# The output's sums of squares and spread roots as products of high and low parts, one dense step later

## The chip, the cores and the metric

The kernel runs on one core of one Trainium2 chip. The metric is device microseconds of one launch, the median of several runs. Beside the runs one execution was profiled; its own time is named beside the median wherever a sum is made from its durations.

## What is computed

One layer of a bidirectional encoder, applied to two requests with the same weights: a prompt of 2048 tokens and a sample of 512, with 16 meta tokens ahead of each. In float32:

```python
def rms_norm(x, g):
    x32 = x.astype(jnp.float32)
    y = x32 * lax.rsqrt(jnp.mean(x32 * x32, axis=-1, keepdims=True) + RMS_EPS)
    return (y * g.astype(jnp.float32)).astype(x.dtype)
...
    u = rms_norm(h, norm_g)
    proj = u @ w_in
    qa, ka, va, za, qb, kb, vb, zb, ga, gb = jnp.split(proj, cuts, axis=-1)
...
    y_a = (o_a * jax.nn.silu(za)) @ w_proj_a
    y_b = (o_b * jax.nn.silu(zb)) @ w_proj_b
    merged = jax.nn.sigmoid(ga) * y_a + jax.nn.sigmoid(gb) * y_b
    return merged @ w_out
...
    h = h + mixer_layer(h, ...)
    return rms_norm(h[:, N_META:], final_g)
```

Here o_a is a neighbourhood attention over a grid of 64 columns and o_b an attention in a window of 128 tokens, each with the meta tokens as extra keys. What matters for the change is the last line: every token's 1024 output features are divided by their root mean square, so that the sum of squares of a token has to be known before any of its features can be written.

## The kernel before, in words

The 2560 tokens are five windows of 512 tokens (w = 0 is the sample, 1 to 4 the prompt). Activations lie feature-major: 128 features on the partitions, 512 tokens along the free dimension, eight such tiles (KT = 8) for 1024 features.

A float32 product is made here in one of two ways. The large ones go through TensorE in its type f32r with both operands split into a high part (a copy that is rounded to f32r) and a low part (the rest): `mm3` at lines 145 to 148 issues high by high, high by low and low by high. `split` (line 251) makes such a pair, ScalarE the high part and VectorE the low one. A few small products are plain f32 (`sums`, line 166, and `spread`, line 181).

First come the input projections, then attention, unit by unit, with dense work in between. Attention units of kind a and of kind b alternate by window: for each window first the 32 units of a, then 16 of b. The unit functions are generators, whose stages are: loads; scores and exponentials (L1111 and L1112 or L1217 and L1218 on TensorE, L1042 on VectorE, L1049 on ScalarE); division by the sum (L1060, L1058); transposes (L1135, or L1237 and L1240) with a split of what they give (L1244, L1245); products with the values (L1150 and L1152, or L1261, L1264 and L1266) and their evacuation (L1268 on ScalarE, the adds of y at L1271 on VectorE). The result of a unit has one PSUM bank (pool ps_o). When a head pair's y is complete, GpSimd multiplies it with the gate (L1274) and it is split into yb (L1066 on ScalarE, L1067 on GpSimd).

The loop over the units (at the end of the kernel) writes out TensorE's order by hand: between the stages `fill` takes so many steps from the queue of dense work. A dense step is the piece of a generator between two `yield`s, six products of 512 columns. The other engines' orders, SP's included, are planned by the compiler's own simulation at build time; `tc.issue_after` puts a limit on that plan.

The dense work of a window w - 1 runs in the units of window w, by `phases` (line 1478): in the a units `dense_pb` and the first half of `dense_out`, in the b units the second half of `dense_out`, then `dense_pa(w)` and, interleaved with it by `with_fill` (line 1470), `dense_fin(w - 1)`. So `dense_fin` runs for four of the five windows. The last window ends otherwise (`finish_end`).

- `dense_pa` and `dense_pb` (lines 1298 and on): psa and psb, the projections of the two branches, eight tiles of two dense steps each. A tile loads its gate (`gated`, line 1293: a DMA on SP into one of three buffers with the tag sg) and multiplies the gate with the PSUM result (ta at L1311). Every two tiles one tile of weights is taken, and the next one is split, the low part on GpSimd (L207, L208).
- `dense_out` (line 1333): pso, the output projection, eight tiles of four dense steps. A tile loads the residual x into an sg buffer (xres), adds it (hT), lets ScalarE square the sum into that same sg buffer and GpSimd add the squares up in one tile ssq of 128 x 512 (L1351, L1353).
- `dense_fin` (line 1355): what is left is the sum over the 128 partitions of ssq, and that goes through TensorE. `sums` uses ssq as weights, 128 tokens at a time, and a column of ones as the moving operand, so that the sums of 512 tokens come out as 128 x 4 (L170). `rsqrt` takes the root by twelve short VectorE instructions (L153 to L163). To bring the roots back to all partitions, `diagonal` (L177) puts each on the diagonal of a 128 x 128 block, and `spread` multiplies by a matrix of ones (L185). ScalarE copies the result to rbs, GpSimd multiplies each of the eight tiles hT with it (L1367), and SP writes them out.

The first piece of `dense_fin` runs with the third dense step of `dense_pa`, then follow five empty steps, then the spread and a tile of the output with each step. TensorE's pool ps_p has three banks with the tag tp; they serve transposes, a third of the a scores, fin_v and rs_rb. The pool d keeps the sg buffers, one buffer with the tag rbs, which holds the diagonal and after it rbs, and one with the tag ssq.

`prep_ahead`, earlier in the kernel, already makes such a sum and spread for other tokens from high and low parts, with `by_ones` (line 188): two products of 512 columns with a matrix of ones as weights (L191, L192).

Of the kernel before, what the change touches and what calls it, by code (L numbers as in the profile page):

```python
# [9 lines left out]
F32 = mybir.dt.float32  # L10
F32R = mybir.dt.float32r
# [6 lines left out]
P = 128  # L18
# [7 lines left out]
WTOK = 512  # L26
# [69 lines left out]
def encoder_block(ctx: ExitStack, tc: tile.TileContext, xT, x_end, w_in, w_pa, w_pb, w_o, norm_g, final_g,  # L96
                  final_row, bias_a0, bias_a1, bias_a2, bias_a3, bias_b, bias_b0, outT_p, outT_s, out_e):
    nc = tc.nc
# [23 lines left out]
    def f32(ap):  # L122
        return ap.bitcast(F32)
# [4 lines left out]
    ones_r = const.tile([P, P], F32R, name="ones")  # L128
# [12 lines left out]
    def move(out, in_):  # L141
        last_move[0] = nc.sync.dma_start(*(f32(a) if a.dtype == F32R else a for a in (out, in_)))
        return last_move[0]
# [6 lines left out]
    def rsqrt(small, sq, m, nc_):  # L150

        ve, hv, r, t = (small.tile([P, 8], F32, tag=f"rs{i}", name=f"rs{i}")[:m, :nc_] for i in range(4))
        nc.vector.tensor_scalar(ve, sq, 1.0 / D_MODEL, EPS, ALU.mult, ALU.add)  # L153
        nc.vector.tensor_scalar(r.bitcast(I32), ve.bitcast(I32), 1, None, ALU.arith_shift_right)
        nc.vector.tensor_scalar(r.bitcast(I32), r.bitcast(I32), -1.0, float(0x5F3759DF), ALU.mult, ALU.add)
        nc.vector.tensor_scalar(hv, ve, -0.5, None, ALU.mult)
        for _ in range(3):
            if nc_ == 1:
                nc.vector.scalar_tensor_tensor(t, r, hv, r, ALU.mult, ALU.mult)
            else:  # L160
                nc.vector.tensor_mul(t, r, hv)
                nc.vector.tensor_mul(t, t, r)
            nc.vector.scalar_tensor_tensor(r, t, 1.5, r, ALU.add, ALU.mult)  # L163
        return r

    def sums(ssq, c0, m, nc_, psum, tag):

        v = psum.tile([P, WTOK], F32, tag=tag, name="fin_v")
        for c in range(nc_):
            nc.tensor.matmul(v[:m, c : c + 1], ssq[:, c0 + c * m : c0 + (c + 1) * m], ones[:, 0:1],  # L170
                             start=True, stop=True)
        return v[:m, :nc_]

    def diagonal(dg, r, m, eng=nc.vector):

        nc_ = r.shape[1]
        eng.tensor_mul(dg[:m, : nc_ * m].rearrange("p (c n) -> p c n", n=m),  # L177
                             ident[:m, None, :m].broadcast_to([m, nc_, m]),
                             r[:m, :, None].broadcast_to([m, nc_, m]))

    def spread(psum, tag, dg, m, nc_):

        rb = psum.tile([P, WTOK], F32, tag=tag, name="rs_rb")
        for c in range(nc_):
            nc.tensor.matmul(rb[:, c * P : c * P + m], ones[:m, :], dg[:m, c * m : c * m + m], start=True, stop=True)  # L185
        return rb

    def by_ones(psum, tag, h, l, name):

        v = psum.tile([P, WTOK], F32, tag=tag, name=name)  # L190
        nc.tensor.matmul(v, ones_r, h, start=True, stop=False)  # L191
        nc.tensor.matmul(v, ones_r, l, start=False, stop=True)  # L192
        return v
# [16 lines left out]
    def split_w(raw, engines=()):  # L210

        wt = wpool.tile([P, 2, KT * P], F32R, tag="wt", name="wt")
        for i, c in enumerate(range(0, KT * P, 4 * P)):
            split_part(wt[:, 0, c : c + 4 * P], wt[:, 1, c : c + 4 * P], raw[:, c : c + 4 * P], *engines[i : i + 1])
        return wt

    class Weights:
# [12 lines left out]
        def split(self, i):  # L230
            if i < len(self.srcs):
                self.wt[i] = split_w(self.raw.pop(i))
# [1045 lines left out]
    pools = {}  # L1278
# [12 lines left out]
    acc = {}  # L1291
# [61 lines left out]
                nc.gpsimd.tensor_add(ssq, ssq, x)  # L1353

    def dense_fin(w):
        r = rsqrt(pools["d"], sums(acc["s", w], 0, P, 4, ps_p, "tp"), P, 4)
        dg = pools["d"].tile([P, WTOK], F32, tag="rbs", name="rs_dg", bufs=1)
        diagonal(dg, r, P)
        for _ in range(5):
            yield  # L1360
        rb = spread(ps_p, "tp", dg, P, 4)
        rbs = pools["d"].tile([P, WTOK], F32, tag="rbs", name="rbs", bufs=1)
        nc.scalar.copy(rbs, rb)
        for f in range(KT):
            hT = acc["h", w, f]
            with tc.issue_after(low[0]):
                nc.gpsimd.tensor_mul(hT, hT, rbs)  # L1367
            dst = outT_s if w == 0 else outT_p
            c0 = 0 if w == 0 else (w - 1) * WTOK
            move(dst[f * P : (f + 1) * P, c0 : c0 + WTOK], hT)  # L1370
            yield
# [106 lines left out]
    def phases(w, br):  # L1478

        if br == "a":  # L1480
            if w == 0:
                yield from islice(gates, GATES_A)
            else:
                yield from dense_pb(w - 1)
                yield from dense_out(w - 1, range(0, 4))
        elif w == 0:
            yield from gates
            open_dense()
            yield from dense_pa(0)
        else:  # L1490
            yield from dense_out(w - 1, range(4, 8))
            pa = dense_pa(w)
            yield from islice(pa, 1)
            yield from with_fill(pa, dense_fin(w - 1))
# [29 lines left out]
    ps_p = ctx.enter_context(tc.tile_pool(name="ps_p", bufs=3, space=PSUM))  # L1524
# [9 lines left out]
    with tc.manual_schedule(engines={E.PE}):  # L1534
# [22 lines left out]
        for i in range(N):  # L1557
            br, w, _, weight = units[i]
# [128 lines left out]
```

## Time and profile before

| | |
|---|---|
| median of 3 runs | 1888.18 us (1886.59 to 1889.76) |
| span of the profiled execution | 1881.7 us |
| TensorE (PE) busy | 1855.9 us, 99% |
| weight loads (PEld) | 1583.0 us, 84% |
| VectorE (DVE) | 1320.6 us, 70% |
| ScalarE (ACT) | 1145.5 us, 61% |
| GpSimd (POOL) | 730.0 us, 39% |
| dense_fin's sums begin at | 1278.35, 1447.54, 1615.05, 1780.16 us |

A row of the order of time gives the start in us from the span's start, the duration, the engine, the line in the code, the operation and the tiles (out<-in), the shapes, and how many like it follow on each other; in brackets stands how long the engine had been idle and what ended that. A matmul's duration is from its start to the modelled end of its way through the array, and the next one starts before that, so TensorE's rate is read from one start to the next. An f32 product of TensorE shows as two instructions, an f32r product as one. In the tile view three numbers are minimum, median and maximum in ns. PEld is TensorE's weight load, which overlaps its matmuls.

### The profile page before, as it was taken

To read this page: it belongs to the slowest core of one execution; us is meant where nothing else is said; L and a number is where in the kernel's file an instruction comes from. 1 tells how busy PE (TensorE), PEld (TensorE's weight loads), DVE (VectorE), ACT (ScalarE), POOL (GpSimd) and SP (SyncE) were. 2 spreads that over 40 slices of the span, in tenths; PEclk is the share of its full clock that TensorE was granted. 3 is DMA by queue.
4 is the path that set the end of the run, shared out by engine and by line. 5 is a ranking of instruction groups with operands and counts; after the bars stand their busy time and mean duration, and the time that the engine had idled before them with its cause. 6 is when DMAs were issued, how large, how long until landed. Compare 5 with 4: busy or idle time off the path is not lost. (4 is left out here: it accounts for less than half of the span.)

```text
span 1881.7 us, 29782 instructions
## 1 busy us (share of the span) xinstructions
PE 1855.9 (99%) x9797; PEld 1583.0 (84%) x9797; DVE 1320.6 (70%) x2961; ACT 1145.5 (61%) x2528; POOL 730.0 (39%) x558
## 2 busy tenths in 40 slices
PE   8999999999999999999999999999999999999998
PEld 6898888888888888888888888888888888888887
DVE  8886657556477565444457888878787887888874
ACT  6454444444365443444456797797789788878932
POOL 2005443323202233322324435656744763685420
PEclk9999999999999999999999999999999999999999
DMA  7667756544296777744258878977985996798383
GB/s 268 234 175 295 207 171 193 211 175 179 84 348 219 235 216 200 209 138 161 104 197 310 273 217 266 304 213 249 316 280 179 320 315 225 222 311 260 119 299 135
DMA packets 290385, 424.83 MB, mean 226 GB/s; under 512 B 117416, under 2 KB 162040, under 8 KB 288696
## 3 DMA queue, kind: packets, MB, share of 16 engines
q1 hardware_dynamic: 289944, 422.93, 69.5%
q8 instruction: 78, 1.28, 0.3%
q14 instruction: 75, 0.61, 0.1%
q10 hardware_dynamic: 288, 0.01, 0.0%
HBM read 303.46 MB, written 119.39 MB: 225 GB/s over the span
## 5 line engine op out<-in xcount | busy, mean ns | idle before, releaser
L208 POOL TENSOR_TENSOR wt<-wraw,wt 128x512 fp32r<-128x512 f32 x164 | 213.1, 1318 | 265.9 <-ACT wt L207 265.8
L848 PE MATMUL pa<-u,wt 128*128 128x512 f32 x1008 | 242.5, 389 | 0.0
L848 PE MATMUL pa<-u,x 128*128 128x512 f32 x984 | 236.9, 390 | 1.2 <-ACT u L859 1.1
L207 ACT CAST wt<-wraw 128x512 fp32r<-128x512 f32 x312 | 177.9, 619 | 74.8 <-PE mm L148 35.3
L848 PEld LDWEIGHTS pa<-u,wt 128*128 128x128 f32 x1008 | 189.0, 188 | 39.2
L848 PEld LDWEIGHTS pa<-u,x 128*128 128x128 f32 x984 | 184.3, 188 | 40.6 <-ACT u L859 2.2
L819 POOL TENSOR_TENSOR s<-wraw,raw 128x512 f32<-128x512 f32 x40 | 58.3, 1458 | 265.5 <-DVE x L208 265.5
L146 PE MATMUL mm<-u,wt 128*128 128x512 f32 (+2 forms) x416 | 150.4, 362 | 7.8 <-ACT u L334 7.2
L814 POOL TENSOR_TENSOR s<-raw 128x512 f32<-128x512 f32 x40 | 58.3, 1456 | 250.0 <-DMA raw<-in_w_in_dram 245.0
L148 PE MATMUL mm<-u,wt 128*128 128x512 f32 (+2 forms) x416 | 146.6, 352 | 2.4 <-DVE wt L208 2.4
L147 PE MATMUL mm<-u,wt 128*128 128x512 f32 (+2 forms) x416 | 146.6, 352 | 1.3 <-DVE u L335 1.3
L208 DVE TENSOR_TENSOR wt<-wraw,wt 128x512 fp32r<-128x512 f32 x148 | 107.2, 762 | 47.2 <-ACT wt L207 47.0
L848 PE MATMUL pe<-u,wt 128*128 128x512 f32 x504 | 121.3, 390 | 0.0
L848 PE MATMUL pc<-u,wt 128*128 128x512 f32 x504 | 121.1, 389 | 0.0
L848 PE MATMUL pe<-u,x 128*128 128x512 f32 x480 | 115.3, 389 | 0.0
L848 PEld LDWEIGHTS pc<-u,wt 128*128 128x128 f32 x504 | 94.6, 188 | 19.6
L848 PEld LDWEIGHTS pe<-u,wt 128*128 128x128 f32 x504 | 94.4, 188 | 19.6
L1139 DVE TENSOR_TENSOR pl<-tp,ph 128x384 fp32r<-128x384 f32 (+6 forms) x160 | 94.8, 593 | 20.2 <-ACT ph L1138 17.7
L1138 ACT CAST ph<-tp 128x384 fp32r<-128x384 f32 (+6 forms) x160 | 81.7, 510 | 43.4 <-PE tp L1135 41.9
L146 PE MATMUL pso<-mh,wt 128*128 128x512 f32 x256 | 107.1, 418 | 0.0
L827 POOL TENSOR_TENSOR s<-wraw,s 128x512 f32<-128x512 f32 x40 | 55.4, 1384 | 131.6 <-DVE wt L208 126.3
L848 PEld LDWEIGHTS pe<-u,x 128*128 128x128 f32 x480 | 90.1, 188 | 18.7
(258 smaller groups left out, 5017.0 us busy)
## 6 DMA issues: line engine op xcount, KB each, us to landing
wraw<-in_w_in_dram SPq DMA_DIRECT2D x86, 512.0 KB
qa<-evq SPq DMA_DIRECT2D x20, 1024.0 KB
raw<-in_w_in_dram SPq DMA_DIRECT2D x40, 512.0 KB
q<-qa SPq DMA_DIRECT2D x20, 1024.0 KB
wraw<-in_w_o_dram SPq DMA_DIRECT2D x32, 512.0 KB
kbt<-kb SPq DMA_DIRECT2D x32, 384.0 KB
qb<-evq SPq DMA_DIRECT2D x20, 512.0 KB
ka<-evk SPq DMA_DIRECT2D x20, 512.0 KB
```

The source lines that it names most:

```text
L146: nc.tensor.matmul(ps, wh, uh, start=first, stop=False)
L147: nc.tensor.matmul(ps, wh, ul, start=False, stop=False)
L148: nc.tensor.matmul(ps, wl, uh, start=False, stop=last)
L207: nc.scalar.copy(h, r)
L208: low[0] = (eng or lo_eng[0]).tensor_sub(l, r, f32(h)).ins
L814: eng.tensor_add(s1, a21, a22)
L819: eng.tensor_sub(s3, a11, a21)
L827: eng.tensor_sub(s4, a12, s2)
L848: nc.tensor.matmul(ps, wt[:, a, s], u[:, b, kk, :], start=first and kk == 0 and i == 0, stop=kk == 3 and i == 2, skip_group_check=True)
L1138: nc.scalar.copy(ph_[:kb, a], tb)
L1139: nc.vector.tensor_sub(pl_[:kb, a], tb, f32(ph_[:kb, a]))
```

## The change

Only `dense_fin` is changed. The sum of squares is split into high and low parts h and l (a copy on ScalarE, a subtraction on VectorE); then a dense step is let pass. The sums are eight f32r products, for each 128 tokens one with h and one with l as weights and two columns of ones as the moving operand, which add up in PSUM. The root is split likewise (128 x 4), each part gets a diagonal of its own, both on VectorE, and after five more steps `by_ones` spreads them with two products of 512 columns. All that follows, the copy to rbs, the products on GpSimd and the output DMAs, comes one dense step later than before. h and the high diagonal take the buffer rbs, the low diagonal that of ssq, and l one of the three sg buffers, in their rotation. rh and rl are two new small tiles.

```diff
     def dense_fin(w):
-        r = rsqrt(pools["d"], sums(acc["s", w], 0, P, 4, ps_p, "tp"), P, 4)
-        dg = pools["d"].tile([P, WTOK], F32, tag="rbs", name="rs_dg", bufs=1)
-        diagonal(dg, r, P)
+        h = pools["d"].tile([P, WTOK], F32R, tag="rbs", name="ssqh", bufs=1)
+        l = pools["d"].tile([P, WTOK], F32R, tag="sg", name="ssql", bufs=3)
+        split(h, l, acc["s", w])
+        yield
+        v = ps_p.tile([P, WTOK], F32, tag="tp", name="fin_v")
+        for c in range(4):
+            for x in (h, l):
+                nc.tensor.matmul(v[:, 2 * c : 2 * c + 2], x[:, c * P : (c + 1) * P], ones_r[:, 0:2],
+                                 start=x is h, stop=x is l)
+        r = rsqrt(pools["d"], v[:, 0:8:2], P, 4)
+        rh, rl = (pools["d"].tile([P, 8], F32R, tag=f"r{x}", name=f"r{x}")[:, :4] for x in "hl")
+        split(rh, rl, r)
+        dh = pools["d"].tile([P, WTOK], F32R, tag="rbs", name="rs_dg", bufs=1)
+        dl = pools["d"].tile([P, WTOK], F32R, tag="ssq", name="rs_dgl", bufs=1)
+        diagonal(dh, f32(rh), P)
+        diagonal(dl, f32(rl), P)
         for _ in range(5):
             yield
-        rb = spread(ps_p, "tp", dg, P, 4)
+        rb = by_ones(ps_p, "tp", dh, dl, "rs_rb")
         rbs = pools["d"].tile([P, WTOK], F32, tag="rbs", name="rbs", bufs=1)
         nc.scalar.copy(rbs, rb)
```

## The prediction

> **What bounds the kernel now.** I read the page first, then the order of time of TensorE around the four places where dense_fin runs, then the tile views of fin_v, and last VectorE, GpSimd and the DMA issues in the same stretches. The page:
>
> ```profile
> span 1881.7 us, 29782 instructions
> PE 1855.9 (99%) x9797; PEld 1583.0 (84%) x9797; DVE 1320.6 (70%) x2961; ACT 1145.5 (61%) x2528; POOL 730.0 (39%) x558
> ```
>
> TensorE bounds the kernel: its order is written by hand and it is busy for 99% of the span. That share proves little alone, as the ends of matmuls are modelled; I go by start to start. The profiled execution has a span of 1881.7 us; the median of the runs is 1888.18, 6.5 us more, which lie around the span. I sum against the span and carry the difference over to the median. Only TensorE time counts in full; work of other engines counts where TensorE then waits for it.
>
> The first dense_fin, in order of time (start, duration, engine, line):
>
> ```profile
> 1277.01 1.28 POOL L1353 TENSOR_TENSOR ssq<-ssq,xres 128x512 f32<-128x512 f32 x1
> 1277.79 0.27 PE L1240 MATMUL tp<-ident,prs 128*32 128x128 f32 x1
> 1278.35 1.05 PE L170 MATMUL fin_v<-ones,ssq 128*128 128x1 f32 x8 [0.29 <-POOL ssq L1353]
> 1279.27 0.47 PE L146 MATMUL psa<-ya,wt 128*128 128x512 f32 x1
> 1279.58 0.39 PE L147 MATMUL psa<-ya,wt 128*128 128x512 f32 x1
> ```
>
> The four f32 products of the sums show as eight instructions, 0.92 us from the first to the next product, 0.11 each. Ahead of them TensorE stands: GpSimd's last sum of squares ends at 1278.29, TensorE starts at 1278.35. The same place in the other three blocks:
>
> ```profile
> 1446.97 0.27 PE L1240 MATMUL tp<-ident,prs 128*32 128x128 f32 x1
> 1447.54 1.02 PE L170 MATMUL fin_v<-ones,ssq 128*128 128x1 f32 x8 [0.29 <-DVE pms L1255]
> 1614.51 0.27 PE L1240 MATMUL tp<-ident,prs 128*32 128x128 f32 x1
> 1615.05 1.02 PE L170 MATMUL fin_v<-ones,ssq 128*128 128x1 f32 x8 [0.26 <-DVE pms L1255]
> 1779.85 0.27 PE L1240 MATMUL tp<-ident,prs 128*32 128x128 f32 x1
> 1780.16 1.05 PE L170 MATMUL fin_v<-ones,ssq 128*128 128x1 f32 x8
> ```
>
> **The wait that goes.** From L1240 to L170 pass 0.56, 0.57, 0.54 and 0.31 us, together 1.98. A transpose needs some 0.11 of that (the L170 instructions' own spacing), so 4 x 0.11 = 0.44 is work and 1.54 us is standing. After the change the sums come one dense step later, that is, after six dense products and the attention work between; in the first block that attention work still runs at 1281.32 (the L1264 row below), so at least 3.0 us lie between GpSimd's end and the sums. In them a ScalarE cast and a VectorE subtraction must run, priced below at 0.62 and 0.76 us. I take the wait as gone: -1.54 us. TensorE now waits for that subtraction, with the next step's six dense products queued behind; if the cover fails, the standing comes back there (rival 1).
>
> **The sums themselves.** They stay eight products with 128x128 weights, now f32r with two columns instead of one. No row before shows that form; what bounds it is the weight load:
>
> ```profile
> L170 PEld LDWEIGHTS fin_v<-ones,ssq x32: 186/192/192, 1278.4 to 1780.9; 128*128 128x128 f32 x32
> L191 PEld LDWEIGHTS fin_v<-xq,ones x2: 188/188/188, 290.7 to 291.1; 128*128 128x128 f32 x2
> 1281.32 0.28 PE L1264 MATMUL ob<-pms,vms 96*64 96x128 f32 x2
> 1281.44 0.28 PE L1266 MATMUL ob<-pl,vb 128*64 128x256 f32 x1
> ```
>
> L170 loads f32 and L191 f32r, both with 128 columns: 192 against 188 ns. So I take 0.11 us each, no change. The other end: the two L1264 products, f32r with weights of 64 columns, take 0.12 together, 0.06 each; at that rate eight save 8 x 0.05 = 0.4 a block, 1.6 in all (rival 2). Above 0.11 I see no reason.
>
> **The spread.** Eight f32 instructions of 128 columns become two f32r products of 512 columns. The kernel has both forms:
>
> ```profile
> 1292.09 1.05 PE L185 MATMUL rs_rb<-rs_dg,ones 128*128 128x128 f32 x8
> 1292.90 0.47 PE L146 MATMUL psa<-ya,wt 128*128 128x512 f32 x1
> 1293.21 0.39 PE L147 MATMUL psa<-ya,wt 128*128 128x512 f32 x1
> 305.49 0.39 PE L191 MATMUL rs_rb<-rs_dg,ones 128*128 128x512 f32 x1
> 305.72 0.40 PE L192 MATMUL rs_rb<-rs_dg,ones 128*128 128x512 f32 x1
> 305.96 0.39 PE L191 MATMUL rs_rb<-rs_dg,ones 128*128 128x512 f32 x1
> ```
>
> From L185 to L147 pass 1.12 us, of which one dense product takes 0.23 (L191 to L192): the spread costs 0.89. The pair at L191 and L192 takes 0.47. Saved: 0.42 a block, -1.68 us for four, all of it on TensorE.
>
> **What is added beside TensorE.** The split of ssq is a cast (L207's kind) and a subtraction (L208's), the split of the root two small ones, and the second diagonal one more L177:
>
> ```profile
> L207 ACT CAST wt<-wraw 128x512 fp32r<-128x512 f32 x312 | 177.9, 619 | 74.8 <-PE mm L148 35.3
> L208 DVE TENSOR_TENSOR wt<-wraw,wt 128x512 fp32r<-128x512 f32 x148 | 107.2, 762 | 47.2 <-ACT wt L207 47.0
> L177 DVE TENSOR_TENSOR rs_dg<-ident,rs x8: 683/689/1683, 26.9 to 1787.3; 128x512 f32<-128x512 f32 x7, 16x16 f32<-16x16 f32 x1
> L153 DVE TENSOR_SCALAR rs<-fin_v x5: 150/156/161, 44.2 to 1781.3; 128x4 f32<-128x4 f32 x4, 128x8 f32<-128x8 f32 x1
> ```
>
> VectorE: 0.76 + 0.16 + 0.69 = 1.6 us a block; ScalarE: 0.62 and a small copy, about 0.16 like L153, 0.8 us. What stands behind them on both engines is the attention's evacuation, and TensorE waits for the adds of y (L1271), since the output of the attention has one PSUM bank:
>
> ```profile
> 1284.00:1290.00 6.00, 6.00 (x40) 5.32 (x39) 5.90 (x14) 3.93 (x11) 2.55 (x2) 1.00 0.46 121
> 1289.73 0.57 DVE L1271 TENSOR_TENSOR y<-ob,ol 64x128 f32<-64x128 f32 x2
> 1290.91 0.28 PE L1261 MATMUL ob<-ph,vb 128*128 128x256 f32 x1
> ```
>
> The columns of the first row are the stretch, its length, and PE, PEld, DVE, ACT and POOL busy. VectorE is full there (5.90 of 6.00), and the adds end at 1290.30, 0.61 us before TensorE wants the bank. But most of the delay is only an exchange: the root's small steps leave that stretch by a dense step, as the sums do, and the diagonals come after 1290. Lower bound 0 (nothing of it is on TensorE), upper bound all of it, 2.4 us a block (rival 3). I take 0, nearest to the quoted 0.61 of cover. The Trainium skill, TensorE: Matmul & The Clock Gate, Architectural detail, calls ScalarE's and VectorE's queues strict first in, first out, which speaks against the change, since a cast that stands early in the queue holds up the rest until ssq is there; no row here can show that cast.
>
> The dependent chain still fits: the spread moves one dense step later together with the sums, and what is put between them (small copy, small subtraction, one diagonal, about 1.0 us) stands against five dense steps, some 14 us (1278.35 to 1292.09).
>
> **What moves.** The spread, the copy of rbs, eight products on GpSimd and eight output DMAs on SP come a dense step later; a step is (1292.09 - 1278.35) / 5 = 2.75 us. No one in the kernel reads the outputs, and the last are due, by fourteen such steps from 1780.16, at about 1819, long before the end. The two halves and the diagonals take buffers (rbs, ssq) whose former content is read before by what they depend on anyway. GpSimd waits for rbs as it does now, only longer:
>
> ```profile
> 1295.84 2.55 POOL L1367 TENSOR_TENSOR hT<-hT,rbs 128x512 f32<-128x512 f32 x2 [8.74 <-ACT rbs L1363]
> 1315.44 1.29 POOL L1067 TENSOR_TENSOR yb<-y,yb 128x512 fp32r<-128x512 f32 x1 [0.79 <-ACT yb L1066]
> 1319.53 0.39 PE L147 MATMUL psb<-yb,wt 128*128 128x512 f32 x1
> ```
>
> Queued behind it are weight splits and the split of yb, which ends at 1316.73 and is wanted at 1319.53: cover 2.80 us against a delay of 2.75. Upper bound one more product ahead of yb, 2.55 / 2 = 1.3 us; lower bound 0, since GpSimd stands for 8.74 us before and can take a split there. I take 0, as even the full delay fits; the other end is rival 4.
>
> The low part l takes a buffer of the gate loads' three. The gate of output tile 1 then cannot be loaded when ssq's tile 6 is done, as now, but after tile 7, at about 1278.3; SP is held there, as it is now for the next gate:
>
> ```profile
> 1278.33 0.89 SPq L142 DMA_DIRECT2D sga<-ga  x2
> 1284.16 0.68 DVE L1311 TENSOR_TENSOR ta<-psa,sga 128x512 f32<-128x512 f32 x1
> DMA packets 290385, 424.83 MB, mean 226 GB/s; under 512 B 117416, under 2 KB 162040, under 8 KB 288696
> ```
>
> It is wanted at 1284.16, 5.8 us later. Even behind a weight tile of 512 KB, 768 KB at the mean 226 GB/s are 3.5 us: cost 0. The gate of tile 3, which follows in l's own buffer, waits for the sums, but its consumer comes four dense steps after 1284.16: cost 0.
>
> **Sum.** 1.54 + 1.68 = 3.2 us less: span 1878.5, median 1888.2 - 3.2 = 1885.0. About 0.2% is what a measurement of this kernel can tell from no change, 3.8 us: the forecast lies just inside.
>
> **Rivals.** (1) A wait takes the old one's place: the subtraction stands behind other VectorE work and l comes late. For it: VectorE is full near by. Against it: 3.0 us for 1.4 us of work. Gain 1.68 only: 1886.5.
>
> (2) The f32r weights load faster: 1.6 us more, 1883.4. The Trainium skill, same page, Weight-path perf modes, has a fast weight load for 128 weights whose type is not FP32, though its table says no win for fp32 widths; the equal 188 and 192 ns speak against it.
>
> (3) The added work lands on TensorE: VectorE and ScalarE are in arrears by 2.4 us a block, the y adds end late, and the bank is not free. It decides once the arrears exceed the cover, 0.61 us in the first block. Price 4 x 2.4 - 3.2 = +6.4: 1894.6, slower. Against it: the exchange above.
>
> (4) GpSimd's delay of a step eats the cover of yb, and one more product of 1.3 us ahead of it lands on TensorE in the three blocks that have attention after them: 3.9 - 3.2 = +0.7: 1888.9.
>
> (5) The order of VectorE, ScalarE and GpSimd is planned anew from the first dense_fin on, and waits elsewhere go:
>
> ```profile
> 1344.23 0.40 PE L1112 MATMUL s<-kd,q 128*128 128x512 f32 x1
> 1345.58 0.52 PE L1135 MATMUL tp<-ident,pr 128*128 128x128 f32 x3 [0.96 <-DVE pr L1060]
> 1355.77 0.40 PE L1112 MATMUL s<-kd,q 128*128 128x512 f32 x1
> 1357.10 0.52 PE L1135 MATMUL tp<-ident,pr 128*128 128x128 f32 x3 [0.93 <-DVE pr L1060]
> ```
>
> Less 0.23 for the product, TensorE stands for 1.12 and 1.10 us. Both gone: 1882.8. Such waits can as well arise.
>
> **Numbers.** Forecast 0.45, rival 1 0.16, rival 2 0.11, rival 3 0.11, rival 4 0.06, rival 5 0.11. Rivals 2 and 5 are faster by over 0.2%, and so is a quarter of the forecast, where a small extra carries it over 3.8 us: 0.11 + 0.11 + 0.11 = 0.33. Rival 3 is slower: 0.11. The rest, 0.56, is within. The range goes from half a microsecond under rival 5, 1882.3, to rival 4, 1888.9; rival 3 and a few points below are left out.
>
> **What would show it.** TensorE from the last transpose to the first product of the next dense step with no standing at dense_fin, sums at 0.11 each and a pair of spread products at 0.47. Standing at the sums with VectorE as releaser shows rival 1; sums at 0.06 rival 2; ob products held by L1271 rival 3; psb held by L1067 rival 4; L1135 waits gone rival 5. The forecast is wrong if the span is not 2.4 to 3.8 us shorter.

## The result and the profile after

The changed kernel takes 1894.11 us (median of 5 runs, 1893.08 to 1896.19), the kernel before 1889.25 beside it (5 runs, 1886.59 to 1890.27): a ratio of 1.0035, interval 1.0022 to 1.0048. By the ratio it is slower by some 6.6 us (the two medians lie 4.9 us apart, 1.0026, which is inside the interval), where 3.2 us less were forecast. The page after:

```profile
span 1891.7 us, 29739 instructions
PE 1861.6 (98%) x9773; PEld 1584.3 (84%) x9773; DVE 1334.0 (71%) x2973; ACT 1148.9 (61%) x2536; POOL 729.2 (39%) x558
```

This execution took 1893.77 us, 2.1 us more than its span. The profiled execution of before (span 1881.7) was thus a quick one, near 1884, and the 10.0 us between the two spans overstate the loss. Single profiles scatter, too: over all 20 kernels, the stretch up to the first pso, ahead of everything that was changed, ends between 1194.3 and 1200.0 us. Where the 10.0 us lie, cut at the first product of psa, psb and pso of each window (sums over the blocks, in us; worked out from the traces' starts):

| stretch | before | after |
|---|---|---|
| up to the first pso | 1194.3 | 1195.7 |
| dense_fin: psa to psb, 4 blocks | 160.2 | 163.5 |
| units of a: psb to pso, 3 | 126.5 | 128.7 |
| pso to psa, 4 | 324.4 | 326.0 |
| from the fourth block's psb to the end | 76.3 | 77.8 |

**The sums came out as forecast.** The order of time of TensorE in the second block:

```profile
1452.58 0.35 PE L1218 MATMUL s<-kbt,q 128*128 128x402 f32 x1
1452.77 0.17 PE L1363 MATMUL fin_v<-ones,ssqh 128*128 128x2 f32 x1
...
1453.46 0.25 PE L1363 MATMUL fin_v<-ones,ssql 128*128 128x2 f32 x1
1453.58 0.48 PE L146 MATMUL psa<-ya,wt 128*128 128x512 f32 x1
```

No standing ahead of L1363, and eight products in 0.81 us. The tile view of fin_v after gives their weight loads (minimum, median and maximum in ns):

```profile
L1363 PEld LDWEIGHTS fin_v<-ones,ssqh x16: 187/192/192, 1282.4 to 1793.3; 128*128 128x128 f32 x16
```

192 ns, as f32 had.

**The spread did not.** The same view, some 14 us later:

```profile
1463.23 0.28 PE L1261 MATMUL ob<-ph,vb 128*128 128x256 f32 x1
1464.15 0.31 PE L1264 MATMUL ob<-pms,vms 96*64 96x128 f32 x2 [0.64 <-DVE pms L1255]
...
1466.79 0.27 PE L1240 MATMUL tp<-ident,prs 128*32 128x128 f32 x1
1468.13 0.47 PE L191 MATMUL rs_rb<-rs_dg,ones 128*128 128x512 f32 x1 [1.07 <-DVE pms L1255]
1468.44 0.39 PE L192 MATMUL rs_rb<-rs_dgl,ones 128*128 128x512 f32 x1
1468.67 0.40 PE L146 MATMUL psa<-ya,wt 128*128 128x512 f32 x1
```

The spread now follows directly on the transposes, and it takes the third of the tp banks, whose last reader, the subtraction that makes pms (L1255; a small tile of the b units, made from a transpose), VectorE has not yet got to. TensorE stands, and the next dense step's products stand behind it. The tile view of pms after counts what waited for it:

```profile
  PE rs_rb L191: 3.7, 3
  PE ob L1264: 1.2, 2
```

3.7 us at the spread in three blocks and 1.2 us at ob in two, where before had 0.6 us at the sums. Time in which TensorE so waits, from one start to the next less the usual spacing, is called a stand below. The stands are 1.65, 1.23 and 1.27 us at the spread, 0.80 and 0.77 at ob, and 0.25, 0.42 and 0.41 at the transposes L1237. The fourth block has none of them, and a stand of 0.63 us that before has there at L1261, behind the y adds (L1271), is gone.

**Why VectorE is late.** Its order in the same block, after (some instructions left out), and GpSimd's:

```profile
1456.05 0.69 DVE L1311 TENSOR_TENSOR ta<-psa,sga 128x512 f32<-128x512 f32 x1
1456.65 1.20 DVE L162 TENSOR_TENSOR rs<-rs,rs 128x4 f32<-128x4 f32 x1
1457.77 1.53 DVE L1060 TENSOR_SCALAR prs<-prs,rd 128x402 f32<-128x402 f32 x1
...
1462.38 0.16 DVE L254 TENSOR_TENSOR rl<-rs,rh 128x4 fp32r<-128x4 f32 x1
1462.45 0.68 DVE L177 TENSOR_TENSOR rs_dg<-ident,rh 128x512 fp32r<-128x512 f32 x1
...
1463.72 0.28 DVE L1255 TENSOR_TENSOR pms<-tp,pms 32x128 fp32r<-32x128 f32 x1
1464.04 0.69 DVE L177 TENSOR_TENSOR rs_dgl<-ident,rl 128x512 fp32r<-128x512 f32 x1
```

```profile
1456.52 2.56 POOL L208 TENSOR_TENSOR wt<-wraw,wt 128x512 fp32r<-128x512 f32 x2 [6.67 <-ACT wt L207]
```

and before:

```profile
1450.80 0.28 DVE L1255 TENSOR_TENSOR pms<-tp,pms 32x128 fp32r<-32x128 f32 x1
1451.12 0.16 DVE L162 TENSOR_TENSOR rs<-rs,rs 128x4 f32<-128x4 f32 x1
...
1454.48 0.43 DVE L1060 TENSOR_SCALAR prs<-prs,rd 128x402 f32<-128x402 f32 x1
```

```profile
1454.84 3.08 POOL L208 TENSOR_TENSOR wt<-wraw,wt 128x512 fp32r<-128x512 f32 x2 [7.45 <-ACT wt L207]
```

One step later the root's chain (the short VectorE instructions L153 to L163, thirteen of them in the trace) falls beside GpSimd's split of the weights. A step of it on 128 x 4 numbers takes 1.20 us instead of 0.16, L1060 1.53 instead of 0.43. GpSimd's two subtractions end at 1457.83 and 1459.07; the step of the chain ends 0.02 us after the first, L1060 0.23 us after the second. Before, the chain was over when the split began, in this block and the third. In the first block it ran beside the split already in before:

```profile
1284.76 1.11 DVE L162 TENSOR_TENSOR rs<-rs,rs 128x4 f32<-128x4 f32 x1
1285.91 1.22 DVE L163 SCALAR_TENSOR_TENSOR rs<-rs,rs 128x4 f32<-128x4 f32 x1
```

There the chain took 4.11 us before and 4.18 after, and before shows no stand of 0.2 us or more behind it: a stretched chain alone does not make TensorE wait. The Trainium skill, SBUF — State Buffer, section SBUF: two separate sides, has the rule: VectorE instructions with two SBUF inputs or in a two-port mode and GpSimd's share a pair of ports under an exclusive lock, held for a whole instruction; the trace agrees, with 1457.85 for the step's end and 1457.83 for GpSimd's. Behind the chain stand the new small split and the diagonals, and pms comes late.

The three blocks in windows, from psa to psb; the columns are the stretch, its length, PE, PEld, DVE, ACT and POOL busy, TensorE's granted clock, the DMA engines' busy share and their GB/s. Before:

```profile
1272.90:1316.30 43.40, 43.11 (x268) 37.71 (x267) 36.92 (x109) 33.32 (x86) 26.72 (x22) 1.00 0.73 242
1441.90:1485.50 43.60, 43.31 (x272) 38.03 (x269) 35.73 (x108) 34.24 (x87) 27.33 (x23) 1.00 0.77 253
1609.50:1652.40 42.90, 42.64 (x272) 37.78 (x269) 34.74 (x108) 33.56 (x86) 27.07 (x23) 1.00 0.75 239
```

After:

```profile
1274.70:1319.50 44.80, 43.23 (x264) 37.25 (x261) 38.95 (x111) 34.59 (x88) 26.39 (x22) 1.00 0.75 243
1444.70:1489.80 45.10, 43.13 (x263) 37.34 (x262) 38.91 (x110) 34.40 (x87) 25.82 (x21) 1.00 0.72 229
1617.30:1662.00 44.70, 42.73 (x266) 37.27 (x263) 38.30 (x110) 34.08 (x88) 25.97 (x21) 1.00 0.72 231
```

TensorE is busy as long as before (129.1 us together in both), the stretches are 4.7 us longer, and VectorE is busy for 116.2 instead of 107.4 us, 8.8 us more: 3 x 1.5 us of added work and, in blocks 2 and 3, 1.0 us more for the chain and 1.1 us more for L1060 each.

**Where nothing was changed.** The stretches from pso to psa hold no dense_fin and no standing, and yet each is 0.3 to 0.4 us longer. The mean spacing of the pso products (640 pairs of starts that follow on each other) is 242.2 ns after, 240.6 before; at the end that of the pse products 209.2 and 203.3. The new small tiles rh and rl lie in the pool d, and pool m, with mh and ml, begins behind it: the two tiles with two buffers of 32 bytes each move mh and ml by 128 bytes per partition, to lower addresses.

### The profile page after: what moved, and what is told of

The parts are those of the page before. It is cut to its first block, busy times and chain, and to the rows that moved or that the text cites. A ratio compares the mean times of both kernels' runs of the same rounds, so it can differ in the third digit from the quotient of the medians.

```text
span 1891.7 us, 29739 instructions
## 1 busy us (share of the span) xinstructions
PE 1861.6 (98%) x9773; PEld 1584.3 (84%) x9773; DVE 1334.0 (71%) x2973; ACT 1148.9 (61%) x2536; POOL 729.2 (39%) x558
## 5 line engine op out<-in xcount | busy, mean ns | idle before, releaser
L208 POOL TENSOR_TENSOR wt<-wraw,wt 128x512 fp32r<-128x512 f32 x164 | 212.1, 1311 | 294.9 <-ACT wt L207 260.1
L208 DVE TENSOR_TENSOR wt<-wraw,wt 128x512 fp32r<-128x512 f32 x148 | 106.1, 755 | 53.8 <-ACT wt L207 53.7
```

What stands on the lines that cost most here:

```text
L208: low[0] = (eng or lo_eng[0]).tensor_sub(l, r, f32(h)).ins
```

## The experiments

Each ratio is to runs of the kernel before on the same chip. "Unshifted" below means this edit, which leaves mh and ml where they lay in before:

```diff
-        rh, rl = (pools["d"].tile([P, 8], F32R, tag=f"r{x}", name=f"r{x}")[:, :4] for x in "hl")
+        rh, rl = (pools["d"].tile([P, 8], F32R, tag=f"rs{i}", name=f"r{x}")[:, :4] for i, x in enumerate("hl"))
```

### The delay alone, and the parts alone

Before, with one empty step ahead of the f32 sums:

```diff
     def dense_fin(w):
+        yield
```

> The sums stay f32 and the spread stays f32; both only come one dense step later. Bank theory (the spread now stands right behind the transposes and needs the third tp bank, whose last reader is the attention's subtraction L1255 on VectorE): the standing at the sums, 1.5 us in all, goes, but the spread stands 1.2 to 1.7 us in each of the first three blocks, together +2 to +3 us against before. Arrears theory (the added VectorE work delays everything that TensorE waits for): VectorE has nothing more to do, so no standing at the spread, and 1.5 us less than before. Theory that the slower time lies outside dense_fin (a planner's new order, the clock): no standing at the spread either, and the stretches behind differ.

1.0027 (1.0015 to 1.0039): most of the loss without any of the new products. The sums' standing goes, but TensorE stands 0.4 us at L1237, 0.31 at L1261 and 0.24 at L1264 in each of three blocks, and the chain takes 4.17 us of VectorE in three blocks where before had 4.11, 2.07 and 2.07. At the spread, where the bank theory wanted 1.2 to 1.7 us, it does not stand. Order of time of TensorE, second block:

```profile
1472.46 0.27 PE L1240 MATMUL tp<-ident,prs 128*32 128x128 f32 x1
1472.57 1.06 PE L185 MATMUL rs_rb<-rs_dg,ones 128*128 128x128 f32 x8
```

So the spread's new place does not make the bank wait by itself. In after VectorE has the added work besides, and takes a score (L1042, 0.55 us) and the y adds (L1271, 0.58 us) ahead of that pms, here behind it; which of the two makes pms late no run separates. dense_fin's four stretches are 1.4 us longer than before, of some 5 us that the ratio gives; in this profile, the slowest of twelve executions (1898.7 us), most of the rest lies in the units of a (136.8 us for 126.5).

Before with only the root's split and the spread in two products, both at their old places:

```diff
-        dg = pools["d"].tile([P, WTOK], F32, tag="rbs", name="rs_dg", bufs=1)
-        diagonal(dg, r, P)
+        split(rh, rl, r)
+        diagonal(dh, f32(rh), P)
+        diagonal(dl, f32(rl), P)
...
-        rb = spread(ps_p, "tp", dg, P, 4)
+        rb = by_ones(ps_p, "tp", dh, dl, "rs_rb")
```

> The sums stay f32 and where they were; only the root is split, and the spread is two f32r products at its old place, behind scores. Bank theory: no standing at the spread, standing at the sums as before (1.5 us in all), so 1.7 us less than before. Arrears theory: the second diagonal and the small subtraction, 0.85 us of VectorE a block, show as standing at the transposes or at L1264, some 0.3 us a block: 0.5 us less than before or no change.

1.0008 (0.9996 to 1.0021). The spread's saving was eaten by stands of 0.55 us at L1237 in each of three blocks and 0.24 at L1264 in the first, and by the moved tiles (below).

After, with four empty steps instead of five, so that spread and outputs keep their step:

```diff
-        for _ in range(5):
+        for _ in range(4):
```

> The whole change, but with four empty steps, so that the spread is at its old place behind scores. Bank theory: no standing at the spread or at the sums; what is left are the 0.4 and 0.8 us at the transposes and at L1264 at most: 1 to 3 us less than before. Arrears theory: those 1.2 us stay in two of the blocks, and with one dense step less the diagonals come late, so that the spread waits for VectorE's L177, 1 us or more a block: slower than before by 0 to 3 us.

1.0027 (1.0017 to 1.0036). The bank's wait is gone, but in the first block the spread waits 0.97 us for the low diagonal, and 0.8 us stays at L1264 and at L1237: the five steps had little to spare for a chain slowed so.

Before with both of these edits, so that only the f32 sums and the root come later:

> The kernel before with the sums one dense step later and four empty steps after them, so that the spread and all behind it keep their place; all in f32, no work added. Port theory (a dense step later the root's short instructions fall under GpSimd's split of a weight tile, where two of them take 1.2 us each in place of 0.16, and VectorE's arrears reach the transposes and products): standing at the sums gone, 0.9 us of standing at tp and ob in each of the first three blocks instead, the a units' stretches as before: 1.000 to 1.0007. Theory that only added work and the later spread matter: the 1.5 us at the sums are gained, 0.999.

1.0009 (1.0000 to 1.0018): the waits at the sums, 1.5 us, are gone, and nothing is gained; the stands at L1237, L1261 and L1264 have taken their place. The sums and the chain moved alone so cost 1.0009, the outputs moved alone 0.9992 (below), and both with the spread 1.0027.

### The bank

```diff
-        rb = by_ones(ps_p, "tp", dh, dl, "rs_rb")
+        rb = by_ones(ps_s, "s", dh, dl, "rs_rb")
```

> The whole change, but the spread writes to a bank of the scores' pool (ps_s) in place of one of the transposes' (ps_p). Bank theory: no standing at the spread (4.2 us less than the changed kernel); 0.4 and 0.8 us at the transposes and L1264 stay: about 0.5 us less than before to 1 us more. Arrears theory: the spread stands just as long, since the diagonals or what lies ahead of them on VectorE are late: no change against the changed kernel, some 5 us over before.

1.0026 (1.0017 to 1.0035). In the second block, order of time of TensorE:

```profile
1469.69 0.27 PE L1240 MATMUL tp<-ident,prs 128*32 128x128 f32 x1
1469.72 0.48 PE L191 MATMUL rs_rb<-rs_dg,ones 128*128 128x512 f32 x1
```

From L1240 to L191 pass 0.03 us, where after has 1.34: the wait was for the bank. The stands at L1237 and L1264 stay. dense_fin's four stretches fall from 163.5 to 159.7 us, but in this profile the units of a rose to 132.0, and the ratio is not told apart from 1.0035: what the bank's wait is worth in time is not shown.

### The outputs

Before with one more step ahead of the eight output tiles:

```diff
         nc.scalar.copy(rbs, rb)
+        yield
```

> The kernel before, sums and spread where they were and f32; only what follows the copy to rbs, the products on GpSimd and the output DMAs, comes one dense step later. Output theory (the stretch of a units behind dense_fin is bound by the DMA engines and SP's queue, and output DMAs that come a step later push its loads): the dense_fin stretches, from the first psa to the first psb, stay at 43.4, 43.6 and 42.9 us, and the stretches from psb to pso behind the second and third, 43.9 and 42.2 us, grow by 1 to 3 us each: 1.001 to 1.002 of before. Theory that the loss is dense_fin's own standing alone: no change anywhere, 1.000.

0.9992 (0.9983 to 1.0001). Before and after with seven of eight output tiles not written:

```diff
-            move(dst[f * P : (f + 1) * P, c0 : c0 + WTOK], hT)
+            if f == 0:
+                move(dst[f * P : (f + 1) * P, c0 : c0 + WTOK], hT)
```

> The kernel before, which writes only the first of the eight output tiles of each of the four blocks, so that 7 MB of output DMAs are left out and those output features stay unwritten. Output theory: the a units' stretches lose most of their standing (1.1, 1.1 and 0.7 us in the profile of before): 2 to 3 us less than before. Otherwise: no change, as nobody waits for an output.

> The changed kernel with the same seven of eight output tiles of each of the four blocks left unwritten. Output theory: what is lost in the a units' stretches goes, and against the kernel before with one output tile only the dense_fin stretches are left, about 3.7 us: 0.2% over that one, where the changed kernel is 0.35% over before. Theory that the loss has nothing to do with the outputs: still 0.3% or more over the kernel before with one output tile.

0.9973 (0.9962 to 0.9983) and 1.0012 (1.0003 to 1.0022). The transfers of the outputs cost some 4 to 5 us, but in both kernels; the difference between them does not shrink without them, and a later start alone shows no cost.

### The moved tiles

Before, with two small tiles in the pool d whose content nothing uses:

```diff
+        for x in "hl":
+            nc.vector.memset(pools["d"].tile([P, 8], F32, tag=f"r{x}", name=f"r{x}")[:1, :1], 0.0)
```

> Before, with two small tiles of 32 bytes (rh, rl, two buffers each) added to the pool d, each touched by one VectorE memset of one element per dense_fin; nothing else. The tiles mh and ml, which lie behind that pool, so move by 128 bytes per partition, as they do in the changed kernel. Theory A (the new tiles shift mh and ml and that slows the products that read them): the mean spacing of the pso products goes from 240.6 to 242.2 ns and that of the pse products from 203.3 to 207.8 ns, as in all profiles of kernels with rh and rl so far; each of the four stretches from the first pso to the next psa gets 0.3 to 0.4 us longer and the end 0.7; ratio 1.0011. Rival (the slower spacing comes from the added instructions or their order, not from the addresses): spacing 240.6 and 203.3, ratio 1.0000.

1.0011 (1.0001 to 1.0022), with spacings of 242.2 and 207.8 ns, and stretches from pso to psa of 326.0 us: what was expected of the addresses. (The spacing at pse is less clean a sign: the delay alone, where nothing was moved, has 207.4.) In the tile view of pso, the high by high products (minimum, median, maximum in ns) of before, then of this kernel:

```profile
L146 PE MATMUL pso<-mh,wt x256: 387/390/487, 1194.3 to 1773.6; 128*128 128x512 f32 x128
```

```profile
L146 PE MATMUL pso<-mh,wt x256: 387/397/486, 1196.8 to 1777.9; 128*128 128x512 f32 x128
```

The other way round, after unshifted:

> After, with rh and rl in the rotation of the root's own small tiles (tags rs0 and rs1) instead of two new tags, so that mh and ml lie where they lay in before. Theory A: pso spacing back at 240.6 ns, pse at 203.3; the standing in dense_fin as in after (the spread behind the transposes 1.2 to 1.7 us in blocks 1 to 3, tp 0.25 to 0.4, ob 0.8); ratio some 0.0011 under after's, 1.0024. Rival (the loss is standing in dense_fin alone): 1.0035.

1.0042 (1.0026 to 1.0058). The pso spacing is back at 240.5 ns, as expected, that of pse at 205.6, not the 203.3 expected, and the time did not follow: new stands, 1.3 us at a score in the units of b and 1.4 us at the end, weigh against it in its profile.

Unshifted and in the other bank together:

> After, with both repairs together: rh and rl in the rotation of the root's own small tiles (mh and ml lie as in before), and the spread in a bank of the scores' pool. Theory (the loss is the sum of the bank wait, of the moved tiles and of VectorE's lateness): no standing at the spread, pso spacing 240.6 ns, the four stretches of dense_fin together about 160 us as in the kernel with the other bank (after: 163.5), tp 0.4 and ob 0.8 left in blocks 2 and 3; ratio 1.0026 - 0.0011 = 1.0015. Rival (the repaired stands only move into the attention units that follow): 1.0030 or more.

1.0023 (1.0012 to 1.0033), dense_fin 160.5 us, and 0.7 and 0.8 us left at L1237 and L1264 in blocks 2 and 3. The bank's wait and the slower pso products are gone, and these stretches are as long as before (160.2 us); by the middle of the interval, more than half of the loss in time is still there.

### VectorE's work, and where the chain lies

The same, with the low part of ssq and the low diagonal on GpSimd:

```diff
-        split(h, l, acc["s", w])
+        nc.scalar.copy(h, acc["s", w])
+        nc.gpsimd.tensor_sub(l, acc["s", w], f32(h))
...
-        diagonal(dl, f32(rl), P)
+        diagonal(dl, f32(rl), P, nc.gpsimd)
```

> The kernel with both repairs (unshifted, other bank), and the low part of the sum of squares and the low diagonal made by GpSimd instead of VectorE. Theory A (the 1.4 us that VectorE does more per block is what TensorE waits for at tp and ob): those stands of 0.4 and 0.8 us in blocks 2 and 3 fall under 0.3, dense_fin's stretches sum to 158.5 us, ratio 1.0005 or less. Theory B (VectorE is late because the root's chain, one step later, runs beside GpSimd's split of the weights, two instructions of it at 1.2 us): the stands stay, the ratio stays at 1.0015.

1.0016 (1.0004 to 1.0027), not told apart from 1.0023. Half of each theory held. The stands at L1237 are gone, so here they hang on the added work (the delay alone has 0.4 us there without it); but the sums wait for GpSimd instead, and ob's stand remains, now in three blocks. Order of time of TensorE, second block:

```profile
1455.03 0.27 PE L1364 MATMUL fin_v<-ones,ssql 128*128 128x2 f32 x1 [0.43 <-POOL ssql L1359]
...
1465.96 0.31 PE L1264 MATMUL ob<-pms,vms 96*64 96x128 f32 x2 [0.60 <-DVE pms L1255]
```

Unshifted, other bank, all on VectorE again, but the sums two steps later and four empty steps behind them, so that only the sums and the chain move, by one more step:

```diff
         split(h, l, acc["s", w])
         yield
+        yield
...
-        for _ in range(5):
+        for _ in range(4):
```

> The kernel with both repairs (unshifted, other bank), the sums two dense steps later instead of one and then four empty steps instead of five, so that the spread and the outputs stay where they are. Theory B (VectorE is late because the root's chain falls beside GpSimd's split of the weights, which stretches two of its instructions or L1060 to 1.2 to 1.5 us): the chain, now behind that split, takes 2.1 us in all four blocks, ob's stand of 0.8 us in blocks 2 and 3 is gone, dense_fin's stretches sum to 158.5 us or less, ratio 1.0023 - 0.0008 = 1.0015. Rival (the added work itself makes VectorE late, wherever the chain lies): the stand stays, or returns at the spread, which now comes 4 steps behind the sums; ratio 1.0023.

0.9998 (0.9986 to 1.0011), against 1.0023 (1.0012 to 1.0033) with the chain a step earlier: the two intervals do not overlap, though barely. The profiles show 2.2 of these 0.0025 x 1888 = 4.7 us, in dense_fin; the two profiled executions themselves took 1890.17 and 1889.89 us, so they do not show where the rest was gained. VectorE (some instructions left out) and TensorE in the second block:

```profile
1457.10 1.47 DVE L1060 TENSOR_SCALAR prs<-prs,rd 128x402 f32<-128x402 f32 x1
...
1460.14 0.28 DVE L1255 TENSOR_TENSOR pms<-tp,pms 32x128 fp32r<-32x128 f32 x1
```

```profile
1463.22 0.28 PE L1261 MATMUL ob<-ph,vb 128*128 128x256 f32 x1
1463.34 0.28 PE L1264 MATMUL ob<-pms,vms 96*64 96x128 f32 x2
```

The chain takes 2.0 us in blocks 2 and 3, pms is done 2.9 us ahead of its use, and ob does not stand. L1060 still runs under GpSimd's split (1.47 us): the one slowed instruction makes no stand at ob here, where it and the slowed chain together did. dense_fin takes 158.3 us. Not all came as expected: in the first block the chain still runs beside GpSimd (3.97 us), and there are two new stands, 0.7 us at the sums of block 1 and 0.85 at L1237 of block 2.

### What stays beside it

After, unshifted, with l in the buffer of ml's eighth tile instead of an sg buffer:

```diff
-        l = pools["d"].tile([P, WTOK], F32R, tag="sg", name="ssql", bufs=3)
+        l = pools["m"].tile([P, WTOK], F32R, tag="ml7", name="ssql")
```

> After, unshifted as before, with the low part l of the sum of squares in a buffer that is free in that stretch (the one of ml's eighth tile) instead of one of the three sg buffers, the spread in its own bank again. Theory (the gate loads are late because the DMA queues are full, not because l holds one of their buffers): the standing of the attention units of a (tp behind L1060, in its turn behind VectorE's wait for the gate at L1326) and the ratio as in the kernel that is only unshifted, 1.0024 to 1.0042. Rival (l's hold of an sg buffer sets the loads back): VectorE's waits for gates in the two stretches under 5 us together (after 8.0, before 7.2), ratio 0.0010 lower.

1.0031 (1.0022 to 1.0041). The ratio alone does not decide: it is inside the theory's range, but also 0.0011 under that of the kernel that is only unshifted, and those intervals overlap. VectorE's waits for gates in the units of a are 7.6 us, 8.0 in after, where the rival wanted under 5: l's buffer was not the cause. The delay alone, and the change unshifted and in the other bank, each with seven of eight outputs left out:

> Before with one empty step at the start of dense_fin, and of each of its four blocks' eight output tiles only the first written (the other seven are computed and left out). To be read beside the kernel before with the same output tiles left out (0.9973). Theory B (what the delay alone costs beyond its standing in dense_fin, 1.3 us or 0.07%, comes from the outputs' transfers meeting the loads of the attention units that follow): 0.9980, and the stretches of the a units behind blocks 1 and 2 at 41.5 us. Rival (the delay's cost does not need the outputs): 0.9973 + 0.0027 = 1.0000, or those stretches at 43 us and more.

> The kernel with both repairs (unshifted, other bank), and of each of dense_fin's four blocks' eight output tiles only the first written (the other seven are computed and left out). To be read beside the kernel before with the same tiles left out (0.9973) and after with them left out (1.0012). Theory (bank wait, moved tiles and VectorE's lateness are the whole loss, the rest is the outputs' transfers meeting the gate loads): dense_fin's stretches 160.5 us as with the outputs, against 160.1 in before; ratio 0.9975 to 0.9982. Rival (something else is lost): 0.9990 or more.

0.9989 (0.9980 to 0.9998) and 1.0010 (1.0001 to 1.0018), against 0.9973 for before without them. The second is the rival's; the first lies between the theory's 0.9980 and the rival's 1.0000, with the rival's stretches at 43.6 and 42.9 us. In these profiles most of the loss that is left lies in the units of a, 126.9 and 129.1 us against 123.4. How a stand arises there, in VectorE and TensorE after:

```profile
1517.93 0.69 DVE L1326 TENSOR_TENSOR sgb<-psb,sgb 128x512 f32<-128x512 f32 x1 [2.68 <-DMA sgb<-gb]
...
1519.20 0.61 DVE L1060 TENSOR_SCALAR pr<-s,rd 128x384 f32<-128x384 f32 x1
```

```profile
1517.71 0.40 PE L1112 MATMUL s<-kd,q 128*128 128x512 f32 x1
1519.96 0.52 PE L1135 MATMUL tp<-ident,pr 128*128 128x128 f32 x3 [1.85 <-DVE pr L1060]
```

VectorE waits 2.68 us for a gate load (L1326), the normalisation (L1060) comes behind that, and TensorE waits 1.85 us for the normalisation. The DMA engines are full there in every kernel: from 10 us before to 25 us after the start of the stretches behind blocks 1 and 2 their busy share is 0.98 to 1.04, and they move 291 to 322 GB/s, from one profile to the next. In all 20 profiles, the stretch behind block 2 took 41.5 to 45.1 us, mean 42.5, in the seven kernels whose sums keep their step, and 42.5 to 47.5, mean 44.5, in the thirteen where they come later. Behind block 1 the same two groups have means of 44.0 and 44.1 us, within 41.5 to 48.8, and one profile per kernel does not settle 2 us here. Whether the later sums lengthen the units of a, and why, stays open.

The version that the runs pointed to: before with the spread in two products at its old place, unshifted, in the other bank; then the same with the outputs a step later:

> Before with the root's split and the spread from two parts at its old place (sums in f32 and no added step), rh and rl in the rotation of the root's own small tiles, and the spread in a bank of the scores' pool. Theory (the spread saves 4 x 0.42 us where VectorE has no more to do than before and mh, ml are not moved): pso spacing 240.6, stands in dense_fin at most 0.25 us a block besides the sums' own, ratio 0.9992 to 0.9996. Rival (0.85 us more VectorE work per block lands on TensorE wherever the spread's bank is): stands of 0.5 us and more per block, ratio 1.0000 or above.

> The spread in two parts at its old place and in the other bank, mh and ml unmoved, the sums as before (measured at 0.9999), and the output tiles one dense step later, as alone gave 0.9992. Theory (the outputs' start leaves more room for the loads of the first attention units): 0.9985 to 0.9992, faster than both kernels. Rival (that difference was scatter): 0.9999.

0.9999 (0.9988 to 1.0009) and 1.0005 (0.9996 to 1.0014). Neither beats before: in the first, of four times 0.42 us, 0.56, 0.30 and 0.24 us come back at L1237 and L1264 in three blocks.

## Why the prediction was wrong

- **The waits at the sums** are gone, and the sums cost 0.11 us a product: both as forecast. The casts and subtractions are priced nearly right (0.62 us, and 0.69 for 0.76), the weight load of f32r is 192 ns, so rival 2 is false.
- **The spread** was nearly right in size: from L191 to the next dense product pass 0.54 us (1468.13 to 1468.67), for a forecast of 0.47, against 0.89 before; it saves 0.35 a block, not 0.42.
- **The step that failed** is "Lower bound 0 ..., upper bound all of it, 2.4 us a block. I take 0". It leaned on one stretch, the first block's, and on the y adds (L1271). That stretch, with VectorE busy for 5.90 of 6.00 us, was full with two steps of the chain that already took 1.11 and 1.22 us beside GpSimd there; what the same would do to the other blocks was not asked. The wait arose at other readers of the same queue, pms and the transposes, and mostly in blocks 2 and 3: 0.25, 1.22 and 1.18 us at L1237 and L1264, together 2.65. "Only an exchange" was the wrong sentence: in these two blocks the chain left a place where it cost 2.07 us and went to one where GpSimd stretches it to 3.1 and L1060 by 1.1 more, and both stand ahead of pms. That the chain's place matters is shown by the pair 1.0023 and 0.9998; that stands of this size arise without any added work, by the delay alone (0.95 us in each of three blocks, 1.0027).
- **What was not in the sum at all**: the spread's new place. Its form was priced, not that it goes directly behind the transposes and asks for a PSUM bank that VectorE has yet to empty. 1.65 + 1.23 + 1.27 = 4.15 us, in three blocks; that it is the bank is shown by the other bank, that the place alone does not do it by the delay alone, so VectorE's lateness, which was taken at 0, is part of this term as well. As the gains are 1.5 + 1.4 us, dense_fin should be 4.15 + 2.65 - 2.9 = 3.9 us longer; it is 3.3, and the stand of 0.63 us that is gone from the fourth block makes up the difference.
- **Nor the tiles that move**: two tiles of 32 bytes, each with two buffers, and the products on mh and ml get slower, 1.6 us in the four stretches from pso to psa, and 1.0 us in the end of the padded kernel. In time, 1.0011 (1.0001 to 1.0022) there; that undoing it shortens after's time was not shown.
- **Rival 3** named the place in principle (VectorE's arrears land on TensorE) and its time, 1894.6, is near the measured 1894.1, but the agreement is partly luck: it priced 2.4 us of added work in each of four blocks, at the y adds; the runs show 6.8 us of stands in three blocks, none of them at the y adds, and the rest of the loss outside dense_fin. Rivals 1 and 4 did not happen. Of rival 5, the waits at L1135 did change: the two quoted ones shrank from 0.96 and 0.93 us to 0.43 and 0.69, but one of 1.85 arose, in all 3.0 us for 2.4.
- **The outputs and GpSimd a step later** at 0, and l in a gate buffer at 0: both hold (0.9992; with l elsewhere the waits for gates stay).
- The difference of 6.5 us between span and median was not work around the span, 2.1 us is, but a quick execution; it did not enter the difference.

Shown, then: whose bank the spread waits for, where the stands at pms come from, and that moved tiles slow the pso products; in time, of these, the chain's place (1.0023 to 0.9998) and, just clear of its interval, the moved tiles. Open: what the bank's wait costs in time, what makes VectorE late for it, and the remaining microseconds, which the profiles put in the units of a.

## What to carry to other kernels

An instruction that is moved has to be priced at its new place: which engine it then shares a port with, which bank it then asks for, and who stands behind it in the queue. An engine that is 70% busy on average can be the one that decides in the stretch where the change is made; count there who reads its results next, not only the nearest one. And a tile added to a pool moves every tile behind it: compare the spacing of products that the change never touched.

## What the runs showed of the hardware

- A VectorE instruction on 128 x 4 f32 numbers took 1.2 us instead of 0.16 beside a GpSimd subtraction of 1.3 us. It goes the other way too: in before, the first of the two L208 at 1454.84 took 1.83 us beside VectorE's diagonal, the second 1.29.
- TensorE's spacing for 512 columns went from 240.6 to 242.2 ns on average when the moving operands lay 128 bytes per partition lower, with nothing else changed but eight one-element writes and the other tiles that moved along.
- After TensorE had stood idle for 1.85 us, up to 1519.96, its granted clock was at half for 3.41 us. The columns of the window are as above, the last but two the clock:

```profile
1519.00:1524.00 5.00, 4.04 (x17) 3.53 (x18) 3.90 (x11) 4.07 (x9) 2.70 (x3) 0.66 1.02 374
```

  Of the 17 places in the units of a where the profiles show 2.0 us and more from one start to the next, six, all of 2.25 us and more, were followed by such a spell; no shorter one was. The Trainium skill, TensorE: Matmul & The Clock Gate, Part 1: The HAM clock gate, asks for an idle window of about 3.4 us; the length of the spell agrees, the idle time that was enough here is shorter.
